# An encoder trunk on one core: weight splits of 1024 columns instead of 512, and the first attention queries one step earlier

## The chip, the cores and the metric

The kernel runs on one core of one Trainium2 chip. The metric is the device time of one execution in microseconds; the kernel before has a median of 1960.28 us over three runs (1959.76 to 1960.9). The profile is of one further execution of the same program.

## The reference, cut to what matters

Two layers act on 512 tokens of width 1024 in float32. Each layer normalises x, projects it to three token mixers and to three sets of merge gates, and adds the merged result back:

```python
h = rms_norm(x, norm_g)
z = h @ w_in                                   # 1024 -> 14848 columns
y_conv = conv_module(c_glu, c_gate, ...) @ w_conv_out        # 31 taps per channel, LayerNorm, SiLU
y_ret  = retention_branch(r_q, r_k, r_v, r_gate, ...) @ w_ret_out   # 4 heads, both directions
y_attn = window_attention_branch(a_q, a_k, a_v, a_gate, ...) @ w_attn_out   # 16 heads, window 128
g = sigmoid(g_logit + b_gate).reshape(B, S, 3, D)
merged = g[:, :, 0] * y_conv + g[:, :, 1] * y_ret + g[:, :, 2] * y_attn
x = x + merged @ w_out
```

## The kernel before, in words

**Matmuls in three parts.** Every operand of a matmul is split in a high part, rounded to the matrix engine's type, and a low part, the rest. `mm3` (L528) issues three matmuls into one sum: high by high, high by low, low by high. Activations are split by `hilo`: a cast on ScalarE, a subtraction on VectorE. Weights come from HBM in pieces of 128 partitions x 1024 columns (`raw`, L437; four buffers `wraw`) and are split by `split` (L445): ScalarE casts to `wh`, and VectorE subtracts into `wl`. For some weights ScalarE writes the negated rounded value into `wl` instead, and a DMA issued from GpSimd adds the weight to it; these are the pieces of the retention's output projection ("or"), of token-wise projections ("xs") once 24 pieces of a layer have gone by, and the last block of `two` ("a22"). The kernel before splits each piece in two halves of 512 columns, each with a tile of its own in pools of eight `wh` and eight `wl`; `Halves` (L367) puts them together again.

**Kinds of projection.** `columns` (L535) makes one 128-channel block of the output for all tokens: 24 matmuls of 512 columns. `two` (L466) makes two blocks at once from seven products of 12 matmuls of 256 columns, in the manner of Strassen: its operands are blocks of the two weight pieces and four sums of them (VectorE, tiles `ws`), each split like a weight. `tokens` and `tokens256` make token-major results, for values and for the attention's queries; `tokens256` issues 96 matmuls of 256 columns into two PSUM tiles.

**One layer.** `layer` (L668) runs four retention heads, then the attention, then `finish`. `head` (L804) computes queries, keys and values, the decayed scores (eight tiles Ph and Pl of pool `pp`, L831), their product with the values (four PSUM tiles `pv`), the group norm, the transposes of the result and its product with the gate. After heads 1 and 3 the output projection follows, eight calls of `columns` with weights "or" (L891); its operands are the transposed results of both heads, each split by `put` (L859). At fixed places of a head, `filler` (L688) does other work: which, stands in `HEAD_FILL` (L47). R, S, L and K are gates by `two`, C the convolution's input, T its 31 taps on VectorE, G and P single gate columns, V the attention's values and keys (`kv`), W the transposes of the keys, and Q0 the first group of attention queries (`Q`: `tokens256`, then `qk_norm`). In head 3 the entry (3, 1) ends with V0, (3, 2) is W0 alone, and Q0 stands at (3, "o"), between the first and the second column of the projection. The attention then has a list of its own, `ATT_FILL`, with the gates of the attention (AG) among it; each of these holds a tile of pool `th` from its tanh until its product with the attention's result.

**LayerNorm of the convolution.** `conv_stats` (L911) has four steps: the sum over channels, the deviations and their squares, the reciprocal root (step 2) and its spread over all partitions (step 3); steps 2 and 3 run in `finish` among the columns of the attention's output projection (`FIN_FILL`).

**Order.** Nothing is issued as it is written. `Plan` (L160) records every operation with a cost and a priority: the time that PE would have reached by then, plus an offset (`urgency`) that draws some operations forward (splits by 16000 ns, PSUM evictions by 20000) or lets them come later (taps, and the statistics by 15000). `Plan.order` (L260) then gives each engine, at each moment of its own clock, the ready operation with the lowest priority number. Tiles of a pool are handed out in the order in which they were first named, and an operation that needs a new tile is held back until one is free. So a pool's size, a cost and a place in the list all change the order on every engine. All instructions are issued from one line (L342), so that the profile is read by tile names: `ps<-wh,big` is a matmul into a PSUM tile of pool ps from a weight tile and a tile of pool big.

Of the kernel before, what the change touches and what calls it, by code (L numbers as in the profile page):

```python
# [12 lines left out]
F32R = mybir.dt.float32r  # L13
# [5 lines left out]
DEPTH, S, D, P = 2, 512, 1024, 128  # L19
# [5 lines left out]
HALF_TAPS = TAPS // 2  # L25


POOLS = {"big": 12, "pp": 8, "mid": 2, "th": 2, "wide": 2, "pad": 1, "yt": 2, "wraw": 4, "wh": 8, "wl": 8, "ws": 2, "half": 3}
PSUM_POOLS = {"pc": 4, "ps": 4}

KEPT = {"xd": 8, "vd": 8, "rg": 16, "cg": 8, "g0": 8, "g1": 8, "g2": 8, "y": 8, "yc": 8, "og": 4, "oa": 8, "m1": 8, "md": 8}
# [5 lines left out]
NORM_EARLY, EVAC_EARLY, SQUARES_LATE = -15000, -20000, 0  # L37
LOAD_EARLY, SPLIT_EARLY, TAPS_LATE, STATS_LATE = -20000, -16000, 150000, 15000
# [7 lines left out]

HEAD_FILL = {(0, 0): "P6 P7", (0, 1): "R0 R1 C0 T0", (0, 2): "C1 C2 R2 R3",  # L47
             (1, 0): "C3", (1, 1): "C4 C5 T1", (1, 2): "C6 R4", (1, "o"): "R5 C7 L0 L1 L2 S0 S1 S2", (2, 0): "T2 S3", (2, 1): "T3 R6", (2, 2): "T4 K0 K1 R7",
             (3, 0): "T5 K2", (3, 1): "T6 T7 K3 V0", (3, 2): "W0", (3, "o"): "Q0"}


C_A, C_B, C_GATE = 0, 1024, 2048
# [1 line left out]
A_Q, A_K, A_GATE, G_LOGIT = 9216, 10240, 10752, 11776  # L54


BY_DMA = ("xs", "or", "a22")


O_BG, O_CB, O_LG, O_LB, O_DW = 0, 24, 32, 40, 48  # L60
# [5 lines left out]
NSUB = 156  # L66


class View:
# [4 lines left out]
    def __init__(self, tile, chain, ix):  # L74
        self.tile, self.chain, self.ix = tile, chain, ix
# [8 lines left out]
    def __getitem__(self, key):  # L84
        key = key if isinstance(key, tuple) else (key,)
        p = key[0]
        if p != slice(None):
            p = slice(p.start // 64, p.stop // 64)
        return self._then("__getitem__", (key,), self.ix[(p,) + key[1:]])
# [274 lines left out]
        return self.t[k // 4][:, k % 4, :]  # L364


class Halves:  # L367


    def __init__(self, a, b):  # L370
        self.t = (a, b)

    def __getitem__(self, key):
        c = key[1]
        i = c.start // 512
        return self.t[i][:, c.start - 512 * i:c.stop - 512 * i]


class Builder:
    def __init__(self, nc, tc, ctx, io):  # L380
        self.plan = self.nc = Plan(nc)
# [3 lines left out]
        self.ctx, self.tc = ctx, tc  # L385
        for name, bufs in POOLS.items():
            self.pools[name] = Pool(ctx, tc, name, bufs)
# [54 lines left out]
            nc.sync.dma_start(out=raw, in_=self.io["wpk"][i])  # L442
        return raw

    def split(self, src, dma=False):  # L445

        nc = self.nc
        wh = self.tile("wh", [P, 512], F32R)
        wl = self.tile("wl", [P, 512], F32R)
        with nc.urgency(SPLIT_EARLY):  # L450
            nc.scalar.copy(out=wh, in_=src)
            if dma:
                nc.scalar.activation(out=wl, in_=src, func=AF.Copy, scale=-1.0)
                nc.gpsimd.dma_start(out=wl, in_=src, accum_op=ALU.add)
            else:
                nc.vector.tensor_tensor(out=wl, in0=src, in1=wh.bitcast(F32), op=ALU.subtract)
        return wh, wl

    def weights(self, key):
        raw = self.raw(key)  # L460
        dma = key[0] in BY_DMA and len(self.keys) % NSUB > 24
        a, b = self.split(raw[:, 0:512], dma), self.split(raw[:, 512:1024], dma)
        return Halves(a[0], b[0]), Halves(a[1], b[1])


    def two(self, col0, col1, out0, out1, func0=None, func1=None):  # L466
        nc = self.nc
        r0, r1 = (self.raw(("ct", self.l, c)) for c in (col0, col1))
        lo, hi = slice(0, 512), slice(512, 1024)
        left, right = slice(0, H), slice(H, S)  # L470
        hs, ts = (self.hh, self.hl), (self.th_, self.tl_)
        sa, sb = [self.tile("ws", [P, 1024]) for i in range(2)]
        early = lambda: nc.urgency(EVAC_EARLY)

        def add(out, a, b, dma=False):
            with nc.urgency(SUM_EARLY):
                nc.vector.tensor_tensor(out=out, in0=a, in1=b, op=ALU.add)
            return self.split(out, dma)

        def product(p, w, x, row, side, first=False):  # L480
            for j in range(4):
                c = slice(j * P, (j + 1) * P)
                self.mm3(p[:, left], (w[0][:, c], w[1][:, c]), tuple(v[row + j][:, side] for v in x), first and j == 0, j == 3, not first)

        a11 = self.split(r0[:, lo])
        s1 = add(sa[:, lo], r1[:, lo], r1[:, hi])
        s2 = add(sa[:, hi], sa[:, lo], r0[:, lo])
        s3 = add(sb[:, lo], r0[:, lo], r1[:, lo])
        a12 = self.split(r0[:, hi], "a12" in BY_DMA)
        s4 = add(sb[:, hi], sa[:, hi], r0[:, hi], "s4" in BY_DMA)  # L490
        a22 = self.split(r1[:, hi], "a22" in BY_DMA)
        a, b, e = self.pc(), self.pc(), self.third()
        t1, v2, t51 = self.half(), self.half(), self.half()
        product(a, a11, hs, 0, left, True)
        with early():
            nc.scalar.copy(out=t1, in_=a[:, left])
        product(b, s2, ts, 4, right, True)
        with early():
            nc.vector.tensor_tensor(out=v2, in0=b[:, left], in1=t1, op=ALU.add)
        product(e, s1, ts, 0, left, True)  # L500
        with early():
            nc.vector.tensor_tensor(out=t51, in0=e[:, left], in1=t1, op=ALU.add)
        product(a, a12, hs, 4, left)
        with early():
            if func0 is None:
                nc.scalar.copy(out=out0[:, left], in_=a[:, left])
            else:
                nc.scalar.activation(out=out0[:, left], in_=a[:, left], **func0)
        product(b, s3, ts, 0, right)
        with early():  # L510
            nc.vector.scalar_tensor_tensor(out=out1[:, right], in0=b[:, left], scalar=-1.0, in1=t51, op0=ALU.mult, op1=ALU.subtract)
        product(e, s4, hs, 4, right)
        with early():
            nc.vector.tensor_tensor(out=out0[:, right], in0=e[:, left], in1=v2, op=ALU.add)
        if func0 is not None:
            nc.scalar.activation(out=out0[:, right], in_=out0[:, right], **func0)
        product(b, a22, ts, 4, left)
        with early():
            nc.vector.scalar_tensor_tensor(out=out1[:, left], in0=b[:, left], scalar=-1.0, in1=t1, op0=ALU.mult, op1=ALU.subtract)
        if func1 is not None:  # L520
            nc.scalar.activation(out=out1, in_=out1, **func1)
# [389 lines left out]
    def conv_stats(self, step):  # L911

        nc = self.nc
        y = lambda k: self.fetch("y", k, self.tile("yt", [P, S]), step == 0)
        with nc.urgency(STATS_LATE):
            if step == 0:
                cs = self.tile("ws", [P, 2, S])
                self.cs, self.rb = cs[:, 0, :], cs[:, 1, :]
                nc.vector.tensor_tensor(out=self.cs, in0=y(0), in1=y(1), op=ALU.add)
                for k in range(2, 8):  # L920
                    nc.vector.tensor_tensor(out=self.cs, in0=self.cs, in1=y(k), op=ALU.add)
            elif step == 1:
                pm = self.pc()
                self.mm(pm, self.ones, self.cs, True, True)
                for k in range(8):
                    yk = y(k)
                    nc.vector.scalar_tensor_tensor(out=yk, in0=pm, scalar=-1.0 / D, in1=yk, op0=ALU.mult, op1=ALU.add)
                    sq = self.rb if k == 0 else self.tile("pad", [P, S])
                    nc.scalar.activation(out=sq, in_=yk, func=AF.Square)
                    self.keep("yc", k, yk)  # L930
                    if k:
                        nc.vector.tensor_tensor(out=self.rb, in0=self.rb, in1=sq, op=ALU.add)
            elif step == 2:
                self.rstd_diag(self.rb, self.cs)
            else:
                nc.scalar.copy(out=self.rb, in_=self.spread(self.cs))
# [321 lines left out]
```

## Time and profile before

| | |
|---|---|
| median of 3 runs | 1960.28 us (1959.76 to 1960.9) |
| the profiled execution | 1959.06 us, of which its span is 1957.3 us |
| instructions | 32895 |
| granted clock of TensorE, mean | 0.998 |
| moved by DMA | 348.98 MB, 178 GB/s in the mean |

Busy time is the time in which at least one instruction of the engine runs. Matmuls overlap: the next begins before the last one's end, which is modelled, so that one of 256 columns shows as 280 ns though the next starts after some 118. The rate of PE is therefore read from the distance between starts, or from a stretch of the chain of waits and its count. PE is the matrix engine, PEld its weight loads, DVE VectorE, ACT ScalarE, POOL GpSimd and SP the engine that issues most DMAs.

### The profile page before, as it was taken

What the parts mean: (1) busy time and instruction counts of PE and PEld (TensorE: products, weight loads), DVE (VectorE), ACT (ScalarE), POOL (GpSimd) and SP (SyncE); (2) the same over time, 40 slices, a digit from 0 to 9 for tenths busy, and PEclk for the clock granted to TensorE, in tenths of its full rate; (3) what the DMA queues carried; (4) which work ended last, traced back from release to release, by engine and by line L of the source; (5) the groups of instructions that cost most, each with busy time, mean ns of one, the idle gap of its engine ahead of it and who ended that gap; (6) DMA issues with size and microseconds to landing.
All of it is one profiled execution on the core that took longest, in us unless ns stands there. A gap on an engine that the chain in (4) does not pass through costs nothing.

```text
span 1957.3 us, 32895 instructions
## 1 busy us (share of the span) xinstructions
PE 1931.5 (99%) x11812; PEld 1717.1 (88%) x11812; DVE 1694.7 (87%) x3122; ACT 1159.7 (59%) x2230; POOL 230.3 (12%) x284
## 2 busy tenths in 40 slices
PE   8999999999999999999999999999999989999999
PEld 6899999999987888878889999999899878887787
DVE  8989998899987898977688999989999788989772
ACT  5565566556555478854436555655565465789541
POOL 0001011110123010000000010111101240110000
PEclk9999999999999999999999999999999999999999
DMA  6377478765678623488523665787656785234772
GB/s 231 91 212 188 135 221 216 207 168 181 181 180 230 202 77 103 148 273 280 169 87 114 213 167 149 219 212 208 170 177 171 211 218 190 86 100 155 252 268 72
DMA packets 143875, 348.98 MB, mean 178 GB/s; under 512 B 16096, under 2 KB 16352, under 8 KB 143712
## 3 DMA queue, kind: packets, MB, share of 16 engines
q1 hardware_dynamic: 115776, 296.02, 45.2%
q0 software_dynamic: 27936, 50.87, 15.1%
q8 instruction: 92, 1.51, 0.3%
q14 instruction: 71, 0.58, 0.1%
HBM read 237.25 MB, written 58.72 MB: 151 GB/s over the span
## 4 chain that ended last, share of the span: by engine, by line
PE 91%; DVE 3%; issue 3%; DMA 2%; POOL 0%; ACT 0%; SPq 0%; POOLq 0%; DVEq 0%
PE pc L342 57%; PE ps L342 34%; DVE ws L342 1%; DMA wraw<-wpk 1%; DMA oa<-pp 1%; DVE yt L342 1%; POOL qk_r L342 0%; DVE wide L342 0%; DVE pp L342 0%; DMA pp<-cg 0%; DMA wl<-wraw 0%; DVE big L342 0%; DMA big<-xT 0%; DMA yt<-y 0%; DVE mid L342 0%
## 5 line engine op out<-in xcount | busy, mean ns | idle before, releaser
L342 PE MATMUL pc<-big,wh 128*128 128x256 f32 (+1 forms) x4848 | 1150.4, 327 | 9.9 <-DVE big L342 7.8
L342 PEld LDWEIGHTS pc<-big,wh 128*128 128x128 f32 x4848 | 809.2, 188 | 91.7 <-DVE big L342 11.0
L342 PE MATMUL pc<-big,wl 128*128 128x256 f32 (+1 forms) x2424 | 789.2, 327 | 0.0
L342 ACT CAST wh<-wraw 128x512 fp32r<-128x512 f32 x558 | 344.3, 621 | 399.6 <-PE pc L342 255.7
L342 PEld LDWEIGHTS pc<-big,wl 128*128 128x128 f32 x2424 | 455.1, 188 | 37.0 <-DVE wl L342 0.3
L342 DVE SCALAR_TENSOR_TENSOR yt<-pad,prm,yt 128x512 f32<-128x512 f32 x480 | 358.3, 746 | 4.4
L342 PE MATMUL ps<-wh,big 128*128 128x512 f32 (+1 forms) x1152 | 296.8, 346 | 6.8 <-ACT big L342 6.8
L342 DVE TENSOR_TENSOR wl<-wraw,wh 128x512 fp32r<-128x512 f32 x364 | 247.3, 685 | 33.9 <-ACT wh L342 31.1
L342 POOL DMA_DIRECT2D wl<-wraw x194 | 169.4, 900 | 851.1 <-ACT wl L342 498.8
L342 ACT CAST wh<-ws 128x512 fp32r<-128x512 f32 x264 | 162.1, 621 | 157.9 <-PE pc L342 81.2
L342 PEld LDWEIGHTS ps<-wh,big 128*128 128x128 f32 x1152 | 199.7, 189 | 36.2 <-ACT big L342 6.8
L342 PE MATMUL ps<-wl,big 128*128 128x512 f32 (+1 forms) x576 | 199.0, 346 | 0.0
L342 DVE TENSOR_TENSOR wl<-ws,wh 128x512 fp32r<-128x512 f32 x264 | 177.5, 685 | 5.4 <-ACT wh L342 4.5
L342 PE MATMUL ps<-big,wh 128*128 128x256 f32 x832 | 151.3, 279 | 0.0
L342 ACT ACTIVATE wl<-wraw 128x512 fp32r<-128x512 f32 x194 | 122.5, 632 | 15.5 <-PE ps L342 15.5
L342 PEld LDWEIGHTS ps<-big,wh 128*128 128x128 f32 x832 | 127.0, 188 | 0.2
L342 PEld LDWEIGHTS ps<-wl,big 128*128 128x128 f32 x576 | 108.8, 189 | 14.8 <-issue 0.2
L342 PE MATMUL ps<-big,wl 128*128 128x256 f32 x416 | 116.0, 279 | 0.0
L342 DVE TENSOR_TENSOR ws<-wraw 128x512 f32<-128x512 f32 x132 | 86.8, 684 | 15.0 <-DMA wraw<-wpk 14.9
L342 PE MATMUL ps<-big 128*128 128x512 f32 (+2 forms) x448 | 99.5, 345 | 0.1
L342 PEld LDWEIGHTS ps<-big 128*128 128x128 f32 x448 | 81.6, 188 | 16.9 <-DVE sm_m L342 1.0
L342 DVE TENSOR_TENSOR ws<-ws,wraw 128x512 f32<-128x512 f32 x132 | 90.2, 683 | 0.1
(124 smaller groups left out, 2092.5 us busy)
## 6 DMA issues: line engine op xcount, KB each, us to landing
wraw<-wpk SPq DMA_DIRECT2D x312, 512.0 KB, 4.1
wl<-wraw POOLq DMA_DIRECT2D x194, 256.0 KB, 5.2
g<-pp SPq DMA_DIRECT2D x48, 256.0 KB, 3.3
pp<-g SPq DMA_DIRECT2D x48, 256.0 KB, 4.3
rg<-pp SPq DMA_DIRECT2D x32, 256.0 KB, 2.7
pp<-rg SPq DMA_DIRECT2D x32, 256.0 KB, 4.6
yt<-y SPq DMA_DIRECT2D x32, 256.0 KB, 2.9
wide<-toe SPq DMA_DIRECT2D x16, 448.0 KB, 3.4
```

The source lines that it names most:

```text
L342: getattr(getattr(self.nc, op.engine), op.method)(**kw)
```

## The change

- Weights are split 1024 columns at a time: one cast, and one subtraction or one accumulating DMA, where there were two. The pools hold four `wh` and four `wl` of 1024 columns instead of eight of 512; `Halves` goes.
- In `two` the blocks are split in pairs: both halves of the first piece in one split (a11, a12), the sums s1 and s2 in one, s3 and s4 in one. All four sums stay. The seventh block, a22, keeps its split of 512 columns with the accumulating DMA and has a pool of its own, `vh` and `vl`, with one tile each.
- `pp` has seven tiles instead of eight, `th` one instead of two.
- In head 3, Q0 moves from between the first two columns of the output projection to the place ahead of W0.
- Steps 2 and 3 of `conv_stats` are drawn forward like PSUM evictions; steps 0 and 1 stay late.

```diff
-POOLS = {"big": 12, "pp": 8, "mid": 2, "th": 2, "wide": 2, "pad": 1, "yt": 2, "wraw": 4, "wh": 8, "wl": 8, "ws": 2, "half": 3}
+POOLS = {"big": 12, "pp": 7, "mid": 2, "th": 1, "wide": 2, "pad": 1, "yt": 2, "wraw": 4, "wh": 4, "wl": 4, "vh": 1, "vl": 1, "ws": 2, "half": 3}
...
-             (3, 0): "T5 K2", (3, 1): "T6 T7 K3 V0", (3, 2): "W0", (3, "o"): "Q0"}
+             (3, 0): "T5 K2", (3, 1): "T6 T7 K3 V0", (3, 2): "Q0 W0"}
...
-BY_DMA = ("xs", "or", "a22")
+BY_DMA = ("xs", "or")
...
-    def split(self, src, dma=False):
-
-        nc = self.nc
-        wh = self.tile("wh", [P, 512], F32R)
-        wl = self.tile("wl", [P, 512], F32R)
+    def split(self, src, dma=False, n=1024, pool="w"):
+
+        nc = self.nc
+        wh = self.tile(pool + "h", [P, n], F32R)
+        wl = self.tile(pool + "l", [P, n], F32R)
...
     def weights(self, key):
         raw = self.raw(key)
-        dma = key[0] in BY_DMA and len(self.keys) % NSUB > 24
-        a, b = self.split(raw[:, 0:512], dma), self.split(raw[:, 512:1024], dma)
-        return Halves(a[0], b[0]), Halves(a[1], b[1])
+        return self.split(raw, key[0] in BY_DMA and len(self.keys) % NSUB > 24)
...
-        a11 = self.split(r0[:, lo])
-        s1 = add(sa[:, lo], r1[:, lo], r1[:, hi])
-        s2 = add(sa[:, hi], sa[:, lo], r0[:, lo])
-        s3 = add(sb[:, lo], r0[:, lo], r1[:, lo])
-        a12 = self.split(r0[:, hi], "a12" in BY_DMA)
-        s4 = add(sb[:, hi], sa[:, hi], r0[:, hi], "s4" in BY_DMA)
-        a22 = self.split(r1[:, hi], "a22" in BY_DMA)
+        add(sa[:, lo], r1[:, lo], r1[:, hi])
+        add(sa[:, hi], sa[:, lo], r0[:, lo])
+        a11, a12 = halves(r0)
+        s1, s2 = halves(sa)
+        add(sb[:, lo], r0[:, lo], r1[:, lo])
+        add(sb[:, hi], sa[:, hi], r0[:, hi])
+        s3, s4 = halves(sb)
+        a22 = self.split(r1[:, hi], True, 512, "v")
...
-        with nc.urgency(STATS_LATE):
+        with nc.urgency(STATS_LATE if step < 2 else EVAC_EARLY):
```

More of the change, by code (lines that the diff above doesn't have):

```diff
@@ L364, in __getitem__ @@
         return self.t[k // 4][:, k % 4, :]
[L367 to L376, printed above, removed]
 class Builder:
@@ L473, in two, with add, halves @@
         early = lambda: nc.urgency(EVAC_EARLY)
-        def add(out, a, b, dma=False):
+        def add(out, a, b):
             with nc.urgency(SUM_EARLY):
                 nc.vector.tensor_tensor(out=out, in0=a, in1=b, op=ALU.add)
-            return self.split(out, dma)
+        def halves(src):
+            w = self.split(src)
+            return [tuple(v[:, c] for v in w) for c in (lo, hi)]
         def product(p, w, x, row, side, first=False):
```

## The prediction

> **What bounds the kernel now.** I read the page's engine table first, then the waits of PE, the chain of waits, PE's and DVE's timeline where PE stood still, and busy time by stage.
>
> ```profile
> span 1957.3 us, 32895 instructions
> ...
> PE 1931.5 (99%) x11812; PEld 1717.1 (88%) x11812; DVE 1694.7 (87%) x3122; ACT 1159.7 (59%) x2230; POOL 230.3 (12%) x284
> ```
>
> PE is busy for 99% of the span, in 11812 matmuls that the change neither adds to nor shortens. So the change can only win time in which PE is starved, and lose by starving it elsewhere. How fast PE goes when fed stands in the chain of waits:
>
> ```profile
> 564.69 8.48 PE pc L342 x72
> ...
> 869.84 111.00 PE pc L342 x482
> ```
>
> 72 matmuls of 256 columns took 8.48 us, 0.118 each; 482 of 512 columns took 111.00, 0.230 each. The waits of PE (total, times, longest) name who starves it:
>
> ```profile
> PE pc L342 <- DVE big L342: 7.8, 7, 2.6
> PE ps L342 <- ACT big L342: 6.8, 1, 6.8
> ```
>
> The second line is the start of the program, one wait for the first input. The first is the entry into the third stage of each layer's retention, the first column of the second projection (columns, L535, called from L891). Two exact windows around it, pc matmuls alone, then the clock just behind (all engines):
>
> ```profile
> 596.75:612.01 15.26, 9.09 (x28) 5.30 (x28) 0.00 (x0) 0.00 (x0) 0.92 0.69 181
> 1568.26:1583.92 15.66, 8.45 (x28) 5.07 (x28) 0.00 (x0) 0.00 (x0) 0.95 0.68 179
> ...
> 606.75:616.75 10.00, 8.07 (x47) 6.78 (x48) 9.43 (x17) 4.76 (x9) 2.78 (x4) 0.83 0.93 205
> 1578.00:1588.00 10.00, 7.16 (x37) 5.77 (x38) 9.44 (x16) 4.20 (x8) 3.47 (x4) 0.83 0.90 193
> ```
>
> Each window holds 28 matmuls of 512 columns and the 16 transposes of the retention's output:
>
> ```profile
> 1569.38 1.47 PE L342 MATMUL ps<-cst,big 128*128 128x128 f32 x12
> ...
> 607.92 0.50 PE L342 MATMUL pc<-big,wh 128*128 128x512 f32 x1 [1.92 <-DVE big L342]
> ```
>
> 12 transposes take 1.47, so 16 take at most 2.0. Fed, a window would need 28 x 0.230 + 2.0 = 8.4 us; it takes 15.26 in layer 0 and 15.66 in layer 1. Lost: 6.9 + 7.3 = 14.2 us, slow clock inside the windows included. DVE's timeline says why:
>
> ```profile
> 595.53 0.42 DVE L342 TENSOR_TENSOR big<-ps,big 128x256 fp32r<-128x256 f32 x1 [6.93 <-PE ps L342]
> 598.19 0.68 DVE L342 TENSOR_TENSOR pp<-ps,pp 128x512 f32<-128x512 f32 x1
> 603.12 1.88 DVE L342 TENSOR_TENSOR pp<-ps,pp 128x512 f32<-128x512 f32 x3
> 610.26 0.68 DVE L342 TENSOR_TENSOR big<-pp,big 128x512 fp32r<-128x512 f32 x1
> ```
>
> DVE stood idle for 6.93 us until the values of V0 were done, then had all at once: V0's splits, the gate products of the four transposed tiles (598.19 and 603.12) and the low halves of the projection's operands, the last at 610.26 to 610.94. The projection can't finish its first column before that, and PE holds nothing else that is ready.
>
> **The change part by part.**
>
> *Q0 ahead of W0 and of the projection.* Q0 is 4 x 8 x 3 = 96 matmuls of 256 columns: 96 x 0.118 = 11.3 us of work whose operands (hh, hl) have long been there. Its first ps tile is free when the first gate product has read its transposes, at 598.87; from there 11.3 us reach to 610.2, while the last operand comes at 610.94. So the gap of 6.9 to 7.3 us is covered, but for the stretch ahead of 599 and the tail: I leave 0.75 us in each layer. Gain 14.2 - 1.5 = 12.7 us, between 14.2 and 0. Q0 also issues two weight loads on SP, two casts on ACT and two subtractions on DVE, ahead of those of column m = 0, two copies, two squares and two sums, and one power on POOL:
>
> ```profile
> L342 POOL TENSOR_TENSOR qk_r<-qk_v,mhalf 128x16 f32<-128x16 f32 x10 | 33.0, 3299 | 112.4 <-DVE qk_v L342 112.4
> ```
>
> That power now stands 3.3 us long ahead of POOL's DMAs for columns about m = 2 to 4; three columns of weights lie ready (4 buffers less the one in use, 24 x 0.230 = 5.5 us each), so 16.5 us cover it. Eight ACT and eight DVE operations of W0 move back by 11.3 us; the attention that reads them starts eight columns, 44 us, later. The place that Q0 leaves, between columns 0 and 1, needs no filler: columns follow one another at 5.5 us with their operands complete. Cost 0; if that cover fails, the 3.3 us.
>
> Of the lost time some is clock: 0.83 of full speed over the 10 us behind each gap. The Trainium skill (TensorE: Matmul & The Clock Gate, Why this matters for your kernels) asks only for gaps over about 3 us to be avoided. By that rule these gaps, the longest 2.6 us, would cost no clock and the gain would be some 3 us less; the rows at 0.83 say otherwise here, so it gets no chance below, and the windows have the loss in them.
>
> *Splits of 1024 columns.*
>
> ```profile
> L342 ACT CAST wh<-wraw 128x512 fp32r<-128x512 f32 x558 | 344.3, 621 | 399.6 <-PE pc L342 255.7 <-PE ps L342 73.2 <-issue 32.2
> L342 DVE TENSOR_TENSOR wl<-wraw,wh 128x512 fp32r<-128x512 f32 x364 | 247.3, 685 | 33.9 <-ACT wh L342 31.1 <-PE ps L342 1.4
> L342 DVE TENSOR_TENSOR wl<-ws,wh 128x512 fp32r<-128x512 f32 x264 | 177.5, 685 | 5.4 <-ACT wh L342 4.5
> L342 ACT ACTIVATE wl<-wraw 128x512 fp32r<-128x512 f32 x194 | 122.5, 632 | 15.5 <-PE ps L342 15.5
> L342 DVE TENSOR_TENSOR ws<-ws,qk_r 128x1024 f32<-128x1024 f32 x10 | 12.2, 1221 | 2.1 <-POOL qk_r L342 2.1
> L342 ACT ACTIVATE wide<-wide,lg 128x896 f32<-128x896 f32 x8 | 8.4, 1046 | 12.9 <-DMA wide<-toe 12.9
> ```
>
> DVE: (364 + 264) / 2 = 314 pairs of 2 x 0.685 become one of 1.22, 0.15 saved each: 47 us of 1694.7. On ACT a 1024-column cast is worth about 1.05 (the row of 896 has 1.046) for 2 x 0.621. Neither engine carries the chain, so I count 0; the hiding work is PE's 1931.5 us itself.
>
> What it can cost is lead. Take a projection column in the stage where each column follows one call of two() (head 1):
>
> ```profile
> 324.67 0.40 PE L342 MATMUL pc<-big,wh 128*128 128x256 f32 x2
> ...
> 334.56 0.63 PE L342 MATMUL pc<-big,wh 128*128 128x512 f32 x2
> ```
> ```profile
> 326.61 0.86 POOL L342 DMA_DIRECT2D wl<-wraw  x1 [1.71 <-ACT wl L342]
> 327.94 0.86 POOL L342 DMA_DIRECT2D wl<-wraw  x1 [0.46 <-ACT wl L342]
> ...
> DMA to landing us min/median/max: 6.1/6.2/6.2
> ```
>
> A column ends at 324.67, the next begins at 334.56 and reads its low half with its third matmul, at 335.0. The two half DMAs went out at 326.61 and 327.94 and both were down by 327.94 + 6.2 = 334.1. Afterwards four whole buffers serve three splits of two() and one of the column, so the column's split still starts when the last column has ended: cast 1.05 and negation about 1.07 (2 x 0.632 likewise shortened), issue near 327.4. One DMA of 512 KB lands between 5.2 (the median of one of 256 KB, below) and 7.5 us (what the pair took from first issue to last landing) later: 332.6 to 334.9. Both are in time, the second barely: I count 0.5 us in all for 14 such columns.
>
> The Trainium skill (DMA: Bandwidth & Descriptors, Anatomy of one DMA) gives 2.0 us plus bytes over 436 GB/s; by that estimate 256 KB more cost 0.6 us, and the weights come with 1.6 us to spare. The rows' pair is slower than that, so I hold to the rows.
>
> *One buffer for the seventh product's split (vh, vl).* The row over all such DMAs:
>
> ```profile
> DMA to landing us min/median/max: 3.2/5.2/9.8
> ```
>
> The split of the next call can start when the previous seventh product is done, not the sixth: 12 x 0.118 = 1.4 us later. Six products, 8.5 us, are left; cast, negation, issue and a median landing take 0.62 + 0.63 + 0.3 + 5.2 = 6.8. Only landings over 6.9 us stall PE, by up to 2.9; I count 0.5 us, at most 5.
>
> *th one tile.* The last gate of attention waits for the only tile:
>
> ```profile
> 844.89 0.60 ACT L342 ACTIVATE th<-pc 128x512 f32<-128x512 f32 x1
> ...
> 849.42 1.29 DVE L342 TENSOR_TENSOR big<-big,th 128x512 f32<-128x512 f32 x2
> ```
>
> Its tanh, at 844.89 now, must wait until the first of the two products at 849.42 is done (850.1); tanh, two DVE products, cast and subtraction (0.60 + 4 x 0.68 by these rows) end near 853.5, some 1 us later than now. PE is then in the first output column and can take the second: 0.5 us a layer, 1.0 in all, at most 3.
>
> *pp seven tiles.* A head holds eight pp at once (Ph, Pl, L831), so the eighth now waits until pv[3] has used Ph[0].
>
> ```profile
> L342 DVE BATCH_NORM_STATS2 bst<-ps 128x6 f32<-128x512 f32 x32 | 21.7, 693 | 10.1 <-PE ps L342 9.9
> L342 DVE TENSOR_TENSOR pp<-mid,pp 128x512 fp32r<-128x512 f32 x32 | 21.8, 684 | 0.0
> ```
>
> Behind that point PE has 14 matmuls, 3.2 us, for a subtraction of 0.684; no stall. But the four pv end together: three statistics of 0.693 later, 2.1 us in each of 8 heads. The filler behind (at least one two(), 84 x 0.118 = 9.9 us) covers it: 0, at most 17.
>
> *Later statistics steps urgent* (L915).
>
> ```profile
> 866.83 1.01 POOL L342 TENSOR_TENSOR tr_r<-tr_v,mhalf 128x4 f32<-128x4 f32 x1 [23.88 <-DVE tr_v L342]
> ...
> 868.31 0.69 DVE L342 SCALAR_TENSOR_TENSOR pp<-pp,pc 128x512 f32<-128x512 f32 x1 [1.57 <-PE pc L342]
> 868.92 0.87 DVE L342 TENSOR_SCALAR ws<-cst,tr_r 128x128 f32<-128x128 f32 x4
> ...
> 869.84 1.12 PE L342 MATMUL pc<-ws,ones 128*128 128x512 f32 x2 [1.56 <-DVE ws L342]
> ```
>
> tr_r is ready at 867.84; DVE, in order, stands before an operation that waits for PE until 868.31, and PE waits 1.56 for the diagonals behind it. Put first, they come when tr_r is there, and the whole step earlier. Two layers, 3.1 us; PE may now meet the chain too early instead, so I take 1.5, between +3 and -3.
>
> **Sum.** 12.7 + 1.5 - 0.5 - 0.5 - 1.0 = 12.2 us off. The profiled execution took 1959.06 (span 1957.3 and 1.76 around it): 1946.9; the median of the runs stands 1.22 higher, so 1948.1.
>
> **Rivals.**
>
> *Q0 is there but comes too late.* The ps tiles are given in order: if Q0 gets one only after the last gate product (603.12 + 1.88 = 605.0), 4.7 us a layer stay exposed: 1960.28 - 14.2 + 9.4 - 1.5 + 2.0 = 1956. For it: DVE works off the gate products in one late group. Against: one tile is free at 598.87, and half of Q0 needs only one.
>
> *Slower: the 512 KB accumulating DMA.* If it lands later than 335.0 - 327.4 = 7.6 us after issue, PE stands still in each of the 14 columns. At the largest landing seen, 9.8, that is 2.2 x 14 = 31 us: 1948 + 31 = 1979. It eats the gain at 7.6 + 12.2 / 14 = 8.5 us. For it: the pair took 7.5. Against: that pair shared the rings with its own second half and still came in time.
>
> *Slower a little: pp.* If half of the 17 us of the late statistics shows, 1957; all of it, 1965. Against: DVE waits there for PE now, not PE for DVE.
>
> **How the numbers follow.** Forecast 0.68 (1943 to 1953, likeliest 1948.1), late Q0 0.13 (1954 to 1959), late DMA 0.10 (1962 to 1980), pp 0.09 (1955 to 1965). About 0.2%, 3.9 us, is what a measurement of this kernel can tell from none: 1956.4 to 1964.2 is "same". Faster: 0.68 + 0.07 + 0.02 = 0.77; same 0.12; slower, most of the late DMA and some of pp, 0.11. The range runs from all gains and no cost, 1960.28 - 17.3 = 1943, taken as 1942, to 1961, beyond which lie the two slower cases.
>
> **What would show it.** Right: between V0's last matmul and the projection PE runs 96 matmuls of 256 columns; the 7.8 us of waits for DVE big shrink below 2 and no window there falls under a clock of 0.95; DVE is busy for about 1648 us; matmuls stay 11812; POOL issues 130 DMAs. The DMA rival: waits of PE for wl in head 1. The pp rival: waits for the transposes. Wrong altogether: new waits of PE over 10 us in sum.

## The result, and the profile after

The changed kernel has a median of 1949.39 us over four runs (1948.84 to 1950.91); the kernel before, on the same chip, 1960.59 (1959.76 to 1961.76). The ratio is 0.9944, with a 95% interval of 0.9928 to 0.9959: 11.2 us faster, where 12.2 were forecast. The profiled execution took 1950.91 us, its span 1949.1.

The engine table of the page:

```profile
span 1949.1 us, 31620 instructions
...
PE 1928.3 (99%) x11812; PEld 1714.9 (88%) x11812; DVE 1674.3 (86%) x2808; ACT 1091.6 (56%) x1786; POOL 172.5 (9%) x220
```

PE has the same 11812 matmuls and 8.2 us less span. DVE fell by 20.4 us, not by 47. The waits of PE (total, times, longest):

```profile
PE ps L342 <- ACT big L342: 7.4, 1, 7.4
PE pc L342 <- DVE wl L342: 4.5, 4, 1.3
PE ps L342 <- DVE big L342: 1.6, 3, 0.6
PE ps L342 <- DVE pp L342: 0.8, 2, 0.4
PE pc L342 <- DMA wl<-wraw: 0.7, 1, 0.7
PE ps L342 <- DMA wl<-wraw: 0.5, 1, 0.5
```

The 7.8 us of the projection's entry (PE pc <- DVE big) are gone from the list, and so is the wait for the diagonals of the LayerNorm. In their place stands a wait that was not there: 4.5 us for `wl`, the low parts of weights.

**The entry.** First PE's groups by shape between 598.2 and 612.0 us, then two of the stretches of the prediction again (us, PE, PEld, DVE, ACT, POOL busy, clock, DMA share, GB/s), then DVE's last operand of the projection:

```profile
L342 PE MATMUL ps<-wh,big 128*128 128x256 f32 x64 | 11.6, 282 | 0.0
L342 PE MATMUL ps<-wl,big 128*128 128x256 f32 x32 | 9.0, 281 | 0.0
```
```profile
596.75:612.01 15.26, 15.26 (x124) 14.64 (x123) 14.51 (x27) 11.35 (x23) 4.31 (x3) 1.00 0.79 207
606.75:616.75 10.00, 10.00 (x71) 9.29 (x70) 9.30 (x18) 7.03 (x12) 1.46 (x2) 1.00 0.92 229
```
```profile
612.13 0.69 DVE L342 TENSOR_TENSOR big<-pp,big 128x512 fp32r<-128x512 f32 x1
```

Q0's 64 + 32 = 96 matmuls stand in the gap. PE is busy for all of the 15.26 us; in the same stretch of the kernel before it was for 11.20, all its matmuls counted. The clock behind, 0.83 before, is 1.00. DVE is as late as ever with the projection's operands (612.13); PE no longer needs them then.

**The attention.** A new loss begins some 90 us later. DVE and PE in the changed kernel, by time (start, us, and in brackets the idle time before and what ended it):

```profile
713.98 1.22 DVE L342 TENSOR_TENSOR wl<-wraw,wh 128x1024 fp32r<-128x1024 f32 x1
...
748.79 1.22 DVE L342 TENSOR_TENSOR wl<-wraw,wh 128x1024 fp32r<-128x1024 f32 x1
```
```profile
715.25 0.50 PE L342 MATMUL pc<-big,wl 128*128 128x512 f32 x1 [0.95 <-DVE wl L342]
...
750.07 0.50 PE L342 MATMUL pc<-big,wl 128*128 128x512 f32 x1 [1.27 <-DVE wl L342]
```
```profile
700.00:760.00 60.00, 56.86 (x337) 48.33 (x336) 56.12 (x119) 45.24 (x100) 4.63 (x6) 1.00 0.23 78
```

A gate column has its high part and waits for the low one, which is late in DVE's queue. PE is idle for 3.1 of these 60 us, while DVE is busy for 56.12 of them, 94%. DVE's share of the span, 86%, hid that.

### The profile page after: what moved, and what is told of

Its sections match the earlier page's. It is cut to its first block, busy times and chain, and to the rows that moved or that the text cites. A ratio compares the mean times of both kernels' runs of the same rounds, so it can differ in the third digit from the quotient of the medians.

```text
span 1949.1 us, 31620 instructions
## 1 busy us (share of the span) xinstructions
PE 1928.3 (99%) x11812; PEld 1714.9 (88%) x11812; DVE 1674.3 (86%) x2808; ACT 1091.6 (56%) x1786; POOL 172.5 (9%) x220
## 4 chain that ended last, share of the span: by engine, by line
PE 92%; DVE 4%; DMA 2%; issue 2%; ACT 0%; SPq 0%; POOL 0%; POOLq 0%; DVEq 0%
PE pc L342 56%; PE ps L342 35%; DMA wl<-wraw 1%; DVE big L342 1%; DVE pp L342 1%; DMA pp<-m 1%; DVE wl L342 1%; DVE ws L342 1%; DVE yt L342 0%; DVE wide L342 0%; DMA rg<-pp 0%; DMA pp<-g 0%; DMA big<-xT 0%; ACT big L342 0%; SPq L342 0%
## 5 line engine op out<-in xcount | busy, mean ns | idle before, releaser
L342 PE MATMUL pc<-big,wh 128*128 128x256 f32 (+1 forms) x4320 | 1054.1, 332 | 0.1
L342 PEld LDWEIGHTS pc<-big,wh 128*128 128x128 f32 x4320 | 729.3, 188 | 78.7 <-issue 1.4
L342 PE MATMUL pc<-big,wl 128*128 128x256 f32 (+1 forms) x2160 | 715.3, 333 | 5.2 <-DVE wl L342 4.5
L342 ACT CAST wh<-wraw 128x1024 fp32r<-128x1024 f32 x246 | 258.1, 1051 | 393.7 <-PE pc L342 180.3
L342 PEld LDWEIGHTS pc<-big,wl 128*128 128x128 f32 x2160 | 405.0, 188 | 42.6 <-DVE wl L342 5.6
L342 DVE TENSOR_TENSOR wl<-wraw,wh 128x1024 fp32r<-128x1024 f32 x182 | 221.8, 1220 | 25.4 <-ACT wh L342 24.4
L342 ACT CAST wh<-ws 128x1024 fp32r<-128x1024 f32 x132 | 138.7, 1052 | 132.9 <-PE ps L342 53.4
L342 DVE TENSOR_TENSOR wl<-ws,wh 128x1024 fp32r<-128x1024 f32 x132 | 160.5, 1219 | 12.4 <-ACT wh L342 11.4
L342 POOL DMA_DIRECT2D vl<-wraw x66 | 57.5, 872 | 528.0 <-ACT vl L342 446.4
L342 PE MATMUL pc<-big,vh 128*128 128x256 f32 x528 | 97.1, 281 | 0.3 <-DVE pp L342 0.3
```

The lines of the kernel that those rows point to most:

```text
L342: getattr(getattr(self.nc, op.engine), op.method)(**kw)
```

## The experiments

All times are medians; each run of several rounds stands beside runs of the kernel before on its own chip (1960.18, 1959.77, 1958.55 and 1959.33 us in the four sessions). Intervals of a ratio are about 0.0025 wide, some 5 us, so that two kernels differ for sure only where intervals part; where they overlap I say whether the ranges of the runs do. Differences below are of medians; worked out from the ratios they come out up to 1.5 us higher or lower. One caution holds for all: any edit changes the planner's order on every engine, so that a difference of two kernels is a term plus what the new order happens to do.

**Which part gains.** Four kernels: the kernel before with Q0 moved and nothing else; the changed kernel with Q0 back; the changed kernel with all statistics late again; the kernel before with Q0 moved and the statistics early.

```diff
 e1_q0_alone, on the kernel before:
-             (3, 0): "T5 K2", (3, 1): "T6 T7 K3 V0", (3, 2): "W0", (3, "o"): "Q0"}
+             (3, 0): "T5 K2", (3, 1): "T6 T7 K3 V0", (3, 2): "Q0 W0"}
 e2_q0_back, on the changed kernel: the same line, the other way round
 e3_stats_late, on the changed kernel:
-        with nc.urgency(STATS_LATE if step < 2 else EVAC_EARLY):
+        with nc.urgency(STATS_LATE):
 e4_before_q0_stats, on the kernel before: e1's edit, and e3's line the other way round
```

> The kernel before with one edit: Q0 stands ahead of W0 in head 3, nothing else is changed (splits of 512 columns, eight pp, two th, late statistics). Theory A (Q0 filling the gap ahead of the second projection is the gain): the 14.2 us lost in the two windows goes but for about 1, so 1960.6 - 13 = 1947.5 us, and the waits of PE for DVE big fall below 1 us. Rival B (the wider splits, which free VectorE and ScalarE, are what made the kernel faster): less than 4 us, 1957 or more.

> The changed kernel with Q0 put back between the first two columns of the second projection; splits of 1024, the smaller pools and the early statistics stay. Theory A: the gap is back, 1949.4 + 13 = 1962 us, not faster than the kernel before, since the new stalls of PE in the attention (about 9 us in sum over both layers) outweigh the statistics (about 3). Rival B: 1950 to 1954.

> The changed kernel with all four statistics steps late again. If the urgency is worth what the two gaps of 1.56 us and the slow matmuls behind them were (4 us), 1952.5 to 1953.5 us, and PE waits 1.5 us for DVE ws in each layer again. Rival: the gap went because the wider splits leave VectorE more free; then no difference, 1949.4.

> The kernel before with Q0 ahead of W0 and the early statistics, but splits of 512 and the larger pools. Theory A says the splits and pools cost some 5 us net (new stalls in the attention against less at other places): 1960.6 - 13 - 3.5 = 1944 us, faster than the changed kernel. Rival B: the splits gain, so this is slower than 1949.4.

| run | median us (range) | ratio (95%) |
|---|---|---|
| e1, Q0 alone | 1949.63 (1949.59 to 1950.27) | 0.9952 (0.9938 to 0.9965) |
| e2, changed, Q0 back | 1961.24 (1959.6 to 1963.35) | 1.0009 (1.0 to 1.0018) |
| e3, changed, statistics late | 1951.88 (1951.6 to 1954.35) | 0.9964 (0.9952 to 0.9977) |
| e4, Q0 and statistics alone | 1946.19 (1945.37 to 1947.32) | 0.9934 (0.9921 to 0.9946) |

Q0's place is worth 10.5 us from one side (1960.18 - 1949.63) and 11.9 from the other (1961.24 - 1949.39): without it the whole change gains nothing. The early statistics are worth 2.5 us (e3 against the changed kernel) to 3.4 (e1 against e4); in both pairs the intervals overlap, but the ranges don't touch. In e2 and e3 the removed waits are back:

```profile
PE pc L342 <- DVE big L342: 4.3, 7, 0.8
```
```profile
596.75:612.01 15.26, 11.13 (x49) 7.41 (x48) 15.21 (x27) 9.50 (x19) 4.18 (x2) 0.89 0.73 221
606.75:616.75 10.00, 8.28 (x40) 7.07 (x39) 7.68 (x15) 6.33 (x11) 0.00 (x0) 0.66 0.68 192
```
```profile
PE pc L342 <- DVE ws L342: 3.1, 2, 1.6
```

The first three lines are of e2, the last of e3. By name e2 has 4.3 of the 7.8 us, in shorter pieces; by the stretch the whole gap is back, with PE busy for 11.13 of 15.26 us (11.20 in the kernel before) and a clock of 0.66 behind it. And e4, which leaves the wide splits and the smaller pools out, is 3.2 us faster than the changed kernel; its runs' range ends below the other's begin. So the rest of the change costs. Three ways were open: the grain of the instructions (A: a 1024-wide low part is whole too late), the smaller pools (B), the wider DMA (C).

**Which part costs.** On the changed kernel: VectorE's subtraction in two halves (e5), negation and DMA in two halves (e7), everything in two halves (e8). On e4: both smaller pools (e6).

```diff
 e5_low_halves:
-                nc.vector.tensor_tensor(out=wl, in0=src, in1=wh.bitcast(F32), op=ALU.subtract)
+                for c in (slice(0, n // 2), slice(n // 2, n)) if n == 1024 else (slice(0, n),):
+                    nc.vector.tensor_tensor(out=wl[:, c], in0=src[:, c], in1=wh.bitcast(F32)[:, c], op=ALU.subtract)
 e7_dma_halves: the same loop around the negation and the accumulating DMA alone
 e8_all_halves: the same loop around all four
 e6_small_pools, on e4:
-POOLS = {"big": 12, "pp": 8, "mid": 2, "th": 2,
+POOLS = {"big": 12, "pp": 7, "mid": 2, "th": 1,
```

> The changed kernel, with VectorE's 1024-wide subtraction issued in two halves of 512 (casts, DMAs and pools as changed). Theory A (the 3.2 us that the changed kernel lies above the one with Q0 and the early statistics alone is grain: PE waits 4.5 us for DVE wl because the low part comes only when all 1024 columns are subtracted): some 1.2 us less in each layer, 1947 to 1948, and the waits PE pc <- DVE wl below 1 us. Theory B (it is the smaller pools): 1949.4 as changed, or up to 1 us more by DVE's extra instructions. Theory C (it is the wider DMA, whose late landings stall PE three times, 2.0 us): 1949.4.

> The kernel before with Q0 moved and the statistics early (1946.2), and with pp 7 and th 1, but with splits of 512. Theory A (grain) and theory C (the wider DMA): 1946 to 1947; my prediction's own price for th, 1.0 in all and 0 for pp, gives 1947.2. Theory B (the smaller pools are the loss): 1949 to 1950.

> The changed kernel, with the negation and the accumulating DMA of a 1024-wide split in two halves (the cast and VectorE's subtraction stay 1024 wide). Theory C (the 512 KB DMA lands too late): the stalls of 0.89, 0.46 and 0.66 us go, 1947.4. Theories A and B: 1949.4, less at most 0.5.

> The changed kernel with its pools, tiles and order, but every cast, negation, subtraction and accumulating DMA of a 1024-wide split in two halves of 512, half by half. Theories A and C together (width of the instructions, not where the tiles lie): 1946 to 1947.5. Theory B (pools, or that 4 tiles of 1024 columns come free later than 8 of 512): 1949 to 1950.

| run | median us (range) | ratio (95%) |
|---|---|---|
| e5, subtraction halved | 1953.78 (1953.64 to 1955.68) | 0.9972 (0.9961 to 0.9984) |
| e6, e4 with pp 7, th 1 | 1949.21 (1947.21 to 1951.57) | 0.9946 (0.9934 to 0.9958) |
| e7, DMA halved | 1951.95 (1951.02 to 1955.38) | 0.9964 (0.9951 to 0.9976) |
| e8, all halved | 1956.95 (1953.63 to 1959.5) | 0.9987 (0.9977 to 0.9996) |

Theory A, mine, falls: finer instructions in the changed kernel's tiles make it slower by 4.4 us (e5) and 7.6 (e8), though the wait for `wl` on DVE is gone in both. Theory C falls too: e7 takes PE's waits for the accumulating DMA from 1.2 to 0.3 us, and the time does not fall. Theory B is left: the small pools alone bring e4 from 1946.19 to 1949.21, within 0.2 us of the changed kernel. By itself this step is not clear of noise (the intervals of e4 and e6 overlap, and the ranges too, by 0.1 us); the runs of single pools below settle it. The wide splits are then worth nothing that these runs can tell, and that nothing has two sides. Instructions of 1024 columns save 7.6 us against halves in the same tiles (e8 against the changed kernel); the tiles, four of 1024 columns with a pool of its own for the seventh product and the paired sums, cost 7.7 us against eight of 512 with the same grain (e8 against e6). Both pairs have intervals that part.

**Which pool.** e4 with pp 7 alone (e10) and with th 1 alone (e11); and the changed kernel with pp 8 and th 2 as before, the room taken from `vh` and `vl`, so that the seventh product's split takes half of a 1024-wide tile (e9).

```diff
 e10_pp7, on e4: "pp": 8 becomes 7          e11_th1, on e4: "th": 2 becomes 1
 e9_wide_big_pools, on the changed kernel:
-"pp": 7, "mid": 2, "th": 1, ... "vh": 1, "vl": 1,
+"pp": 8, "mid": 2, "th": 2, ...
-        a22 = self.split(r1[:, hi], True, 512, "v")
+        a22 = self.split(r1[:, hi], True, 512)
-        wh = self.tile(pool + "h", [P, n], F32R)
+        wh = self.tile(pool + "h", [P, 1024], F32R)[:, 0:n]
```

> The changed kernel with its wide splits, but th 2 and pp 8 as before: the seventh product's split of 512 takes half of a 1024-wide tile of the common buffers, not a buffer of its own. Theory B (the smaller th and pp are what the changed kernel loses against the kernel with Q0 and early statistics alone, 1946.2): 1946 to 1947. Rival (the wide splits held in 4 buffers cost it): 1949 to 1952, more where the column behind a two() now waits for a buffer.

> The kernel before with Q0 moved and the statistics early (1946.2), and pp 7 alone. My prediction's price for pp is 0: 1946.2. If pp is what the small pools' 3.0 us are: 1949 to 1949.5, with PE's waits in attention.

> The kernel before with Q0 moved and the statistics early (1946.2), and th 1 alone. My prediction's price for th is 1.0 in all: 1947.2, lost at the output projection behind attention. If th is all of the small pools' cost: 1949 to 1949.5.

| run | median us (range) | ratio (95%) |
|---|---|---|
| e9, wide splits, pp 8, th 2 | 1979.55 (1978.18 to 1984.91) | 1.0114 (1.01 to 1.0128) |
| e10, e4 with pp 7 | 1954.74 (1951.91 to 1958.6) | 0.9985 (0.9976 to 0.9994) |
| e11, e4 with th 1 | 1944.84 (1942.52 to 1945.15) | 0.9928 (0.9916 to 0.9941) |

It is pp: one tile fewer costs 8.5 us with th 2 (e10 against e4, whose intervals part) and 4.4 with th 1 (e6 against e11, whose ranges don't touch). One th tile fewer costs nothing: with seven pp tiles it even brings 5.5 us (e6 against e10, whose intervals part), so that what one pool costs depends on the other. e11 is the fastest kernel of all, 4.6 us below the changed one, with ranges that don't touch. e9 says nothing for B, since its new wait is another: four `wl` tiles now serve two() and the column behind it, and PE waits for the late DMA,

```profile
PE ps L342 <- DMA wl<-wraw: 13.8, 9, 2.6
```

where the changed kernel, with a tile of its own for the seventh product, has 0.5 in one wait. So four wide tiles need that extra one.

How pp does it can be followed in part. DVE's groups in layer 0 from 590 to 665 us, e10 first, then e4 and e6 (busy, mean ns, idle time before and what ended it):

```profile
L342 DVE SCALAR_TENSOR_TENSOR pp<-pp 128x512 f32<-128x512 f32 x8 | 5.4, 685 | 2.3 <-DMA pp<-g 2.3
L342 DVE TENSOR_SCALAR yt<-pad,prm 128x512 f32<-128x512 f32 x1 | 0.5, 547 | 4.8 <-DMA pad<-vd 4.8
```
```profile
L342 DVE SCALAR_TENSOR_TENSOR pp<-pp 128x512 f32<-128x512 f32 x8 | 5.5, 684 | 0.0
L342 DVE TENSOR_SCALAR yt<-pad,prm 128x512 f32<-128x512 f32 x1 | 0.5, 540 | 0.0
```
```profile
L342 DVE SCALAR_TENSOR_TENSOR pp<-pp 128x512 f32<-128x512 f32 x8 | 5.5, 684 | 0.0
L342 DVE TENSOR_SCALAR yt<-pad,prm 128x512 f32<-128x512 f32 x1 | 0.5, 533 | 0.0
```

A pp tile is also where gates come back from HBM (`pp<-g`). In e10 DVE waits for one, and for the convolution's last channel block, whose tile `pad` is of another pool. It falls behind with the taps, which it works off when nothing more urgent is there: by the timelines e10 has 62 taps of the layer left at 610 us and e4 61, at 630 us 60 and 53. But e6 has seven pp tiles too and neither wait, so these loads are a part of the matter in e10 alone. Then the attention begins. The last tap and the matmul that waits, in e10, and the same in e11:

```profile
744.35 0.75 DVE L342 SCALAR_TENSOR_TENSOR yt<-pad,prm,yt 128x512 f32<-128x512 f32 x1
```
```profile
744.47 0.47 PE L342 MATMUL ps<-pp,big 128*128 128x512 f32 x1 [4.18 <-DVE big L342]
```
```profile
735.55 0.74 DVE L342 SCALAR_TENSOR_TENSOR yt<-pad,prm,yt 128x512 f32<-128x512 f32 x1
```
```profile
742.32 0.50 PE L342 MATMUL ps<-big 128*128 128x256 f32 x2 [0.33 <-DVE big L342]
```

In e10 a tap stands between nearly every two operations of the attention up to the one PE waits for, 4.18 us; in e11 the taps end at 736 and PE waits 0.33. In e6 they end at 740, behind the start of PE's wait of 2.1 us. In layer 1 the order is the same (last tap of e10 1712 us, of e6 1709, of e11 1699). The wait there, in e10 and then in e6:

```profile
1713.92 0.47 PE L342 MATMUL ps<-pp,big 128*128 128x512 f32 x1 [2.13 <-DVE big L342]
```
```profile
1710.62 0.47 PE L342 MATMUL ps<-pp,big 128*128 128x512 f32 x1 [2.13 <-DVE big L342]
```

So with seven pp tiles this matmul waits 2.13 us in both layers of e6 and in layer 1 of e10, where DVE has no wait for `pp<-g`. Late taps and a late attention on DVE are what the traces show; why one tile fewer makes the taps late, but for the loads in layer 0 of e10, stays open.

The rest of the loss is clock. e6 and e11 differ in pp alone; the profiled execution of e6 is 8.8 us longer (spans of 1949.5 and 1940.7 us; the two lie at the far ends of their runs, hence more than the 4.4 of the medians). PE stands still in it for 5.3 us more, and its 11812 matmuls are busy for 3.5 us more; a clock of 0.83 over the 10 us behind the wait in each layer makes 3.4 of that.

**Taps out of the attention's way.** The last run takes the taps from there, in the changed kernel.

```diff
 e12_taps_earlier
-LOAD_EARLY, SPLIT_EARLY, TAPS_LATE, STATS_LATE = -20000, -16000, 150000, 15000
+LOAD_EARLY, SPLIT_EARLY, TAPS_LATE, STATS_LATE = -20000, -16000, 30000, 15000
```

> The changed kernel with the convolution's taps (yt <- pad) due 30 us after their place in the program instead of 150, so that each layer's last taps stand ahead of attention's first softmax on VectorE. Between 700 and 740 us VectorE is busy for 38.4 of 40 us, 16.4 of them taps, while it had 8.2 us to spare between 560 and 600 and 6.2 between 640 and 680. Theory (what the changed kernel still loses, 4.8 us in each layer in attention, is VectorE full with taps there): most of it goes, 1941 to 1946, no wait of PE for wl over 0.5 us between 700 and 760. Rival (attention's own operations come too late by their order, or the taps are now in the way of the retention's gates): 1949.4 or slower.

It took 1988.22 us (1984.31 to 1990.43; ratio 1.0141, 1.0124 to 1.0158). The stretches of e12 with the taps gone from the first two, and put into the third; then PE's wait, the first gate product on DVE, and the first matmul of Q0:

```profile
700.00:760.00 60.00, 60.00 (x372) 53.47 (x371) 43.87 (x100) 44.64 (x97) 9.71 (x7) 1.00 0.24 80
717.80:777.80 60.00, 59.77 (x363) 52.50 (x362) 46.32 (x109) 47.88 (x105) 6.95 (x7) 1.00 0.21 71
600.00:640.00 40.00, 32.13 (x173) 27.23 (x172) 34.70 (x58) 18.21 (x28) 8.68 (x7) 0.87 0.50 138
```
```profile
615.40 0.80 PE L342 MATMUL pc<-big,wh 128*128 128x512 f32 x1 [3.63 <-DVE big L342]
```
```profile
615.94 0.68 DVE L342 TENSOR_TENSOR pp<-ps,pp 128x512 f32<-128x512 f32 x1
```
```profile
617.28 0.41 PE L342 MATMUL ps<-wh,big 128*128 128x256 f32 x1
```

The local half of the theory is shown: from 700 to 760 us DVE is busy for 43.87 us instead of 56.12, and PE for all 60. The attention begins 17.8 us later in e12 (first `sm_m` of the softmax at 681.8 us instead of 664.0); in the stretch moved by as much, DVE is busy for 46.32 us and PE for 59.77. The rest is wrong by far. The 8 us that DVE had to spare between 560 and 600 are not filled (it is busy there for 26.69 us, less than before); the taps, no longer last in line, stand ahead of the retention's gate products and low halves instead, and PE waits 3.63 us in the projection's first columns, where Q0 had closed the gap. Q0 itself comes too late there: the first gate product, which frees its ps tile, runs at 615.94 us (598.87 in the changed kernel), and its first matmul at 617.28, behind the wait. This is the rival "Q0 is there but comes too late" of the prediction, brought about by the taps. Due times between 30 and 150, or an earlier date for the last block alone, were not tried.

## Why the prediction was right, and which of its steps were not

- **Q0, 12.7 forecast.** Measured 10.5 (e1) and 11.9 (e2). The mechanism is as told: 96 matmuls, no gap, no slow clock (1.00 where 0.95 was named as the sign). The rest is not lost at the entry but, as the lists of waits suggest, given back later: PE's waits on a PSUM tile for DVE's `pp`, 1.8 us in the kernel before, are 3.5 in e1, with 1.1 more for `sm_m` of the softmax.
- **Statistics, 1.5 forecast between +3 and -3.** Measured 2.5 and 3.4. Taking half was too careful: the waits of 2 x 1.56 = 3.1 us went whole. Both gains together are 14.0 us in e4, forecast 14.2.
- **The 512 KB DMA, 0.5.** It lands as bounded, a median of 6.2 us between the 5.2 and 7.5 of the prediction, and the rival that it stalls every column falls. PE waits for it twice, 1.2 us in all (0.5 and 0.7, the list above); removing that (e7) brought no time. POOL issues the 130 DMAs that were named as a sign (64 of 512 KB, 66 of 256 KB). One small sum beside this term is off: a landing of 5.2 + 0.6 us after 327.4 leaves 1.8 us to 335.0, not 1.6; nothing rests on it.
- **The seventh product's buffer, 0.5.** PE has no wait for it in the changed kernel; e9 shows that it earns its place.
- **th, 1.0.** Falls: e11 is 1.3 us faster than e4 (ranges that don't touch, intervals that overlap). The last tanh of layer 0 does wait in e11, 3.0 us, and comes at 846.2 us instead of 840.9, but PE has no wait between 820 and 880 us.
- **pp, 0: the step that failed.** The prediction followed one use of the pool, the eight scores Ph and Pl, and found cover; its rival put the price into the late statistics behind them. The price was 4.4 to 8.5 us, up to the half of that rival's 17 us that the prediction reckoned with, at another place: the taps end later, DVE's operations in the attention with them, and one matmul of each layer waits 2.1 us (4.2 in layer 0 of e10), with a slow clock behind it. Loads that land in pp tiles are a part of it in e10; what else makes the taps late stays open.
- **Splits, 0.** On balance right (0.2 us, the changed kernel against e6, far inside the noise), with the wrong reason: two effects of over 7 us cancel. "Neither engine carries the chain" fits DVE's 87% of the span; in the attention DVE is at 94%, and PE waits there for its low parts.
- **DVE at about 1648 us.** It was 1674.3. The sum took two durations of 0.685 for a pair. DVE's timeline in the kernel before and in the changed one, by start times:

```profile
61.48 0.68 DVE L342 TENSOR_TENSOR mid<-pc,pp 128x512 f32<-128x512 f32 x1
62.09 0.68 DVE L342 TENSOR_TENSOR wl<-ws,wh 128x512 fp32r<-128x512 f32 x1
62.69 0.68 DVE L342 TENSOR_TENSOR mid<-mid 128x512 f32<-128x512 f32 x1
```
```profile
62.75 1.21 DVE L342 TENSOR_TENSOR wl<-ws,wh 128x1024 fp32r<-128x1024 f32 x1
63.88 0.68 DVE L342 TENSOR_TENSOR mid<-mid 128x512 f32<-128x512 f32 x1
```

Each starts before the last one's end: 512 columns come every 0.60 us, 1024 take 1.13 to the next start. A pair becomes cheaper by 0.07, not by 0.15, and 314 x 0.07 = 22 us, near the 20.4 measured. The Trainium skill (VectorE: DVE Perf Modes, The TRN2 errata) gives (N + 151) / 0.96 ns for a float32 operation of N columns, 0.69 and 1.22 us; the durations here agree, but in a queue that is fed their sum isn't the time.

In sum 10.5 + 3.4 of gain, 3.0 of cost for the pools and 0.2 for the splits give 10.7 us (1949.5 from 1960.2), with the changed kernel at 1949.39. That this closes proves nothing, since the four are the steps of one chain of runs (e1, e4, e6, the changed kernel). The forecast of 12.2 came near since the gains, most of the sum, were read from waits of PE that stood in the trace. The costs, 2.0 forecast and 3.2 measured, came near by luck: th and pp were wrong in opposite directions.

## What to carry to other kernels

Work that is ready and waits for nothing is worth most where the critical engine waits for a late group of another engine: moving it there brought all of the change, and the finer edits around it only moved the next wait. An engine's share is read per stage, at the place where the edit will be felt: 87% of the span was 94% in the attention. Before a pool loses a tile, list every user of its tiles, the loads that land in them too: here the price of one tile came at none of the places that had been looked at. And what a filler gets by being last in line is lost when it is made urgent.

## What the runs showed of the hardware that was not expected

The clock of PE falls after waits that are short. In e6 PE stands still for one wait of 2.13 us and two of 0.23 and 0.24 right behind it, and the matmuls that follow run at half clock for some us; e4 has at the same place four waits of under 1 us each. First e6, its wait and three stretches behind it, then e4:

```profile
741.60 0.47 PE L342 MATMUL ps<-pp,big 128*128 128x512 f32 x1 [2.13 <-DVE big L342]
```
```profile
741.60:744.60 3.00, 2.53 (x9) 1.83 (x10) 3.00 (x8) 2.86 (x9) 0.00 (x0) 0.81 0.31 87
744.60:746.80 2.20, 2.20 (x8) 1.81 (x8) 1.70 (x7) 1.35 (x4) 0.00 (x0) 0.50 1.00 343
746.80:749.00 2.20, 2.20 (x16) 1.86 (x14) 1.67 (x6) 1.20 (x3) 0.00 (x0) 0.99 0.51 190
```
```profile
738.00:748.00 10.00, 8.09 (x42) 6.10 (x43) 9.91 (x30) 7.81 (x21) 0.38 (x2) 1.00 0.44 144
```

The clock is 0.81 in the mean over the 3.0 us behind the wait, 0.50 over the next 2.2, and full again after. 0.19 x 3.0 + 0.50 x 2.2 = 1.7 us of full speed are lost behind a wait of 2.1, so that it costs nearly twice what the list of waits says. In layer 1 of e6 the same wait is followed by the same 0.83 over 10 us. In e4 10 us with 1.9 us of idle time in pieces keep the full clock. The Trainium skill (TensorE: Matmul & The Clock Gate, What's actually happening) tells of a free-running window of about 3.4 us and of a clock of either half or full speed; 1.7 us lost at half speed make 3.3 us of it, which agrees. Its section Why this matters for your kernels asks for gaps of no more than about 3 us; here 2.13 us, with two short waits behind it, were enough, and the measurement decides. That 2.13 us alone would do is not shown.
